# Up projection of a gated feed-forward in split float32: three matmuls per K tile, or two with the high limb of the weights over both limbs of the activations

## The chip, the cores and the metric

One NeuronCore of a Trainium2 chip runs the whole kernel in one launch. The metric is device microseconds of that core. The kernel before has a median of 1290.29 us over 3 runs (1290.16 to 1291.49).

The engines are named as in the profile: PE is TensorE (PEld its weight loads), DVE is VectorE, ACT is ScalarE, POOL is GpSimd, SP is SyncE, which here only issues DMAs.

## The reference

One layer of a hybrid attention block for 256 latent tokens and 256 context tokens of width 2048: modulation, RMSNorm, an input projection into three groups of heads, an output projection with a gated residual, then the feed-forward that matters here:

```python
h2 = rmsnorm(x, g_ffn[l]) * (1 + sc2) + sh2          # [256, 2048]
u  = h2 @ w_up[l]                                     # [256, 11264]
u  = sum(pad(u)[:, j:j + L] * conv_w[j] for j in range(3)) + conv_b   # along the tokens
gate, val = split(u, 2, axis=-1)
x  = x + gt2 * ((silu(gate) * val) @ w_down[l])       # [256, 2048]
return rmsnorm(x, g_final)
```

All inputs and the output are float32.

## The kernel before, in words

Every large matrix product is done in two limbs. `split` (L116 to L123) rounds a tile to float32r as its high limb H (ACT, L119) and takes the rest as its low limb L (DVE, L120). `mm3` (L107 to L114) then sums three products into one PSUM bank: H·H, H·L and L·H, with the first letter for the stationary side. Each of the three is a matmul of its own with a weight load of its own.

Weights arrive as raw tiles of 1 MB over SP's queue. `take` (L177 to L194) hands out a quarter of a raw tile in limbs and splits the quarters up to `look[0]` = 4 ahead of use; there are six buffers for such quarters (L161). Large tiles (raw weights, h2, gates, x2, the activations) share 16 buffers named b8 (L66). `mm3` also keeps a pace: after so many columns it calls `fill` (L272), which brings in one more 512 KB piece of the late modulation weights over POOL's queue (L217, some of them held back by a small POOL copy, L212), adds an earlier piece into a running sum on DVE (L230, L232: one pass over 128x1024), and, when a block of 16 pieces is done, sums it over the partitions on PE (L256 or L266 and L267).

Before the feed-forward, `h_cols` makes h2 from x2: transposed, scaled by gain and (1 + sc2), in limbs, but without the 1/rms of the token and without the shift. The shift stands as two more columns (L775), so that the up projection runs over 258 columns: 256 tokens and the shift's own product. `rb_make` (L782) spreads 1/rms over all partitions by two small matmuls (L787) and a copy.

The up projection has 88 column tiles of 128; a pair of them (gate and value) makes 128 columns of the activation. Per column tile there are 16 K tiles, and per K tile one `mm3` over 258 columns (L802), so 48 matmuls per column tile and 4224 in all. The first two pairs run together, K quarter by K quarter over four column tiles (`UP_FIRST`). `up_act` (L806) then takes a pair: the shift's column is copied out (DVE, L812), the product is multiplied by 1/rms (DVE, L813) and shifted (ACT, L814), convolved with three taps (L816 to L818), and silu and the product of the two halves follow (L820, L821). `store` splits the result into limbs of `act`.

The 44 pairs go in four chunks of 16, 12, 8 and 8; after each chunk the down projection takes its rows with `mm3` over 512 columns (L882). The pieces of modulation weights that are left at the feed-forward, for the second gate, are brought in during the first chunk's pairs and, at a faster pace, during its down projection; the first two column blocks of that need half of them, the last two need all (`fill_to`, L865 and L872).

The order of the instructions on each engine is fixed when the program is built, by priority and readiness, and need not be the order in which they are written.

Of the kernel before, what the change touches and what calls it, by code (L numbers as in the profile page):

```python
# [7 lines left out]
F32 = mybir.dt.float32  # L8
# [6 lines left out]
P = 128  # L15
# [13 lines left out]
UP_FIRST = 2  # L29
H_AT = 2  # L30
# [6 lines left out]
def _columns(*parts):  # L37
    """columns of the packed vectors"""
    at, o = {}, 0
    for n, w in parts:  # L40
        at[n] = (o, o + w)
        o += w
    return at, o
# [8 lines left out]
def block_kernel(ctx: ExitStack, tc: tile.TileContext, a, out):  # L52
# [54 lines left out]
    def mm3(ps, lH, lL, rH, rL, first, last, skip=False):  # L107
# [3 lines left out]
        pace[1] += pace[0] * 3 * rH.shape[-1] * 0.427e-3  # L111
# [4 lines left out]
    def split(H, L, src, scale=None):  # L116
        """H = src (* scale) rounded to float32r, L = the rest."""
# [26 lines left out]
    pace = [0.0, 0.0]  # how fast the column groups of the late mod parts follow the matrix products, and how many are due  # L144
# [10 lines left out]
    kept = [("d", (lo // 4 + q) * 4 + 3) for q in range(n // 4 - 1)]  # the last column block: rows one half after the other  # L155
# [21 lines left out]
    def take(key, i):  # L177
        """limbs of a quarter of a weight tile; later quarters are split ahead"""
# [21 lines left out]
    b2v = const.tile([P, 2, KT], F32, name="b2v")  # sh2 | sc2, per partition  # L200
# [6 lines left out]
    def m2_dma(n):  # L207
        if m2["dma"] >= len(M2):
            return
        with ExitStack() as held:  # L210
            if m2["dma"] < 4 or m2["dma"] >= 96:  # not ahead of the weights of the stage
                hold = pool.tensor_copy(tiny(1, "hold"), recent[0][:, 1, 0:1].bitcast(F32)).ins  # L212
                held.enter_context(tc.issue_after(hold))
# [7 lines left out]
    def m2_acc(flush=False):  # L221
        """what the last group brought, behind the limbs made last"""
# [14 lines left out]
    def m2_end(blk, acc):  # L237
        """limbs of a finished gate sum now, the sum over the partitions with the next group"""
# [68 lines left out]
    def mod1_mm(g):  # L307
        """sums for sh1 | sc1 of K-tile g of the stream, a quarter of the sum in every 32 rows"""
# [64 lines left out]
    # keys of the neighbourhood heads, and the first half of c_kv  # L373
# [11 lines left out]
    def proj_T(key, ps, both, part=None):  # L385
        """columns of w_in as the stationary side: [128 columns, tokens]"""
# [9 lines left out]
    def proj_N(kind, toks):  # L396
        """tokens as the stationary side: [128 tokens, 512 columns]"""
# [12 lines left out]
    # values of the neighbourhood heads  # L410
# [4 lines left out]
    # the rest of c_kv, and the rotary key  # L415
# [19 lines left out]
    # c_kv normed, in limbs  # L435
    def kv_rms():
        """1/rms of c_kv's tokens, on the diagonals of four blocks"""
# [35 lines left out]
    def softmax(S, e, scale_ap=None):  # L473
        """rows of S (PSUM or SBUF), scaled, -> their softmax"""
# [25 lines left out]
    # c_q: gain applied, in limbs; its 1/rms goes into the scale of the scores' rows  # L500
# [37 lines left out]
    # queries of the neighbourhood heads; every softmax stands between dense products  # L538
# [24 lines left out]
    # Fourier mixing  # L563
# [51 lines left out]
    # latent heads: values of four heads, queries and keys of two  # L615
# [52 lines left out]
    # the output projection's first column block starts beside the last heads  # L668
# [65 lines left out]
    def x2_cols(nb, t, gate, ss=None):  # L734
        """x2 += gate * the product, for a block of columns; sums of squares on the side"""
# [7 lines left out]
    def h_cols(nb):  # L743
        """columns of x2, transposed, gain and scale applied, in limbs; 1/rms waits until after the up projection"""
# [49 lines left out]
    def up_mm(n):  # L794
        """tiles n of the up projection, K in quarters over all of them"""
        pss = [bank() for _ in n]
        for q in range(4):
            for i, ps in zip(n, pss):
                w = take(("u", i), q)
                for k in range(4):  # L800
                    kt = 4 * q + k
                    mm3(ps[:, : SEQ + 2], w[:, 0, k * P : (k + 1) * P], w[:, 1, k * P : (k + 1) * P],  # L802
                        *hsl(h2, kt, 0, SEQ + 2), kt == 0, kt == KT - 1)
        return pss

    def up_act(j, pss):  # L806
        cv = []
        for s in range(2):
            ps = pss[s]
            c = conv[:, 2 * j + s, :]  # L810
            ub = tiny(1, "ub")
            dve.tensor_copy(ub, ps[:, SEQ : SEQ + 1])  # L812
            dve.tensor_tensor(ps[:, :SEQ], ps[:, :SEQ], rb, ALU.mult)  # L813
            act.activation(ps[:, :SEQ], ps[:, :SEQ], AF.Identity, bias=ub, scale=1.0)  # L814
# [9 lines left out]
    def finish(t):  # L824
        """1/rms, and the last columns' gain, on the rows of x2"""
# [13 lines left out]
    for ci, (lo, n) in enumerate(chunks):  # L839
        last = ci == len(chunks) - 1  # L840
        at = [b8([P, 2, 4, SEQ], F32R, s="act") for _ in range(n // 4)]
        pend = []

        def store():
            i, v = pend.pop(0)
            split(at[i // 4][:, 0, i % 4, :], at[i // 4][:, 1, i % 4, :], v)

        j = lo
        while j < lo + n:
            g = UP_FIRST if j == 0 else 1  # L850
            pss = []
            if g > 1:
                pss = up_mm(range(2 * j, 2 * j + 2 * g))
                rb_make()
            else:
                pss = up_mm([2 * j]) + up_mm([2 * j + 1])
            for i in range(g):
                v = up_act(j + i, pss[2 * i : 2 * i + 2])
# [35 lines left out]
def _layout(i):  # L894
# [5 lines left out]
    def vec(v):  # [n * 128] -> [128, n]  # L900
        return v.reshape(-1, P).T

    def tiles_k(w, k):  # [K, N] -> [K / (128 k), 128, k * N]: k K-tiles of all N columns
# [3 lines left out]
    def tiles_n(w):  # [K, N] -> [N / 128, 128, K]: all K of 128 columns  # L907
# [33 lines left out]
    # relative bias of every (head, column, row offset, key column); -1e30 outside the window  # L941
# [58 lines left out]
```

## Time and profile before

| | |
|---|---|
| median of 3 runs | 1290.29 us (1290.16 to 1291.49) |
| span of the profiled execution, first to last instruction | 1286.6 us |
| PE busy / weight loads | 1251.4 us (97%) / 1129.4 us (88%) |
| DVE busy | 982.8 us (76%) |
| ACT busy | 699.7 us (54%) |
| POOL busy | 115.0 us (9%) |
| mean granted TensorE clock | 0.994 |
| first and last matmul of the up projection | 523.1 us, 1231.4 us |

The page lists the span of the profiled execution and no device time of its own; the median stands 3.7 us above that span. Times are microseconds from the span's start. A matmul's record is longer than the distance to the next one, since matmuls are pipelined; what a matmul costs in a dense stretch is read from the distance between starts, that is from how many begin in a window. The same holds in a small way for DVE, whose records overlap by less than 0.1 us.

### The profile page before, as it was taken

The page shows a single profiled execution, that of the slowest core. Times are in us where ns is not written, and L with a number is a line of the kernel's source. Part 1 is how long each engine was busy: PE and PEld are TensorE (multiplying, and loading weights), DVE is VectorE, ACT ScalarE, POOL GpSimd, SP SyncE. Part 2 cuts the span into 40 slices and gives each one's busy share as a digit, 9 for nine tenths or more (in the row PEclk, how much of TensorE's full clock was granted, in tenths as well). Part 3 has the DMA queues.
Part 4 walks back from the last instruction along what each step waited for, and adds up shares of the span by engine and source line. Part 5 has one row for each costly group of instructions (what it writes and reads, how often), then busy time and mean ns, then how long its engine had stood idle before and what let it go on. Part 6 is the DMA issues. An engine that isn't in the chain of part 4 may idle for free.

```text
span 1286.6 us, 22194 instructions
## 1 busy us (share of the span) xinstructions
PE 1251.4 (97%) x8688; PEld 1129.4 (88%) x8688; DVE 982.8 (76%) x1805; ACT 699.7 (54%) x1327; POOL 115.0 (9%) x177
## 2 busy tenths in 40 slices
PE   5999989999999999999999999999999999999996
PEld 4888869998887888999999788999988999899985
DVE  5444588999989788798988956778766778777785
ACT  5333323765555555576666544666654566456662
POOL 0000121111111013212111100000000000000000
PEclk9999989999999999999999999999999999999998
DMA  9998688776756977766666657544455645554521
GB/s 384 419 404 317 233 291 313 239 251 240 246 196 250 363 279 293 306 255 236 227 229 230 229 196 290 184 149 164 169 192 209 243 141 193 190 207 160 189 107 66
DMA packets 53657, 304.96 MB, mean 237 GB/s; under 512 B 6064, under 2 KB 7216, under 8 KB 26800
## 3 DMA queue, kind: packets, MB, share of 16 engines
q1 hardware_dynamic: 34256, 234.37, 48.8%
q0 software_dynamic: 18432, 67.12, 15.2%
q10 hardware_dynamic: 864, 2.05, 0.4%
q8 instruction: 68, 1.11, 0.3%
q14 instruction: 37, 0.30, 0.1%
HBM read 301.42 MB, written 2.10 MB: 236 GB/s over the span
## 4 chain that ended last, share of the span: by engine, by line
PE 92%; DMA 3%; DVE 2%; ACT 1%; issue 1%; POOL 0%; DVEq 0%; POOLq 0%; ACTq 0%
PE ps L108 27%; PE ps L110 26%; PE ps L109 26%; PE g L108 2%; PE ms L314 2%; DMA wm<-in_wm_dram 2%; PE g L109 2%; PE g L110 2%; PE ps L489 1%; PE ps L360 1%; DMA sm<-in_small_dram 1%; DVE acc L232 1%; DVE hl L120 1%; PE ps L256 1%; ACT hl L119 0%
## 5 line engine op out<-in xcount | busy, mean ns | idle before, releaser
L119 ACT CAST hl<-raw 128x512 fp32r<-128x512 f32 (+2 forms) x732 | 443.6, 610 | 397.6 <-PE ps L110 315.7
L120 DVE TENSOR_TENSOR hl<-raw,hl 128x512 fp32r<-128x512 f32 (+2 forms) x732 | 486.4, 676 | 161.1 <-ACT hl L119 155.7
L108 PE MATMUL ps<-h,hl 128*128 128x258 f32 x1408 | 398.5, 283 | 0.0
L109 PE MATMUL ps<-h,hl 128*128 128x258 f32 x1408 | 396.2, 281 | 0.0
L110 PE MATMUL ps<-h,hl 128*128 128x258 f32 x1408 | 395.8, 281 | 0.0
L109 PEld LDWEIGHTS ps<-h,hl 128*128 128x128 f32 x1408 | 266.5, 189 | 0.2
L110 PEld LDWEIGHTS ps<-h,hl 128*128 128x128 f32 x1408 | 265.8, 189 | 0.0
L108 PEld LDWEIGHTS ps<-h,hl 128*128 128x128 f32 x1408 | 265.4, 189 | 0.2
L232 DVE SCALAR_TENSOR_TENSOR acc<-wm,c,acc 128x1024 f32<-128x1024 f32 x120 | 153.3, 1277 | 8.4 <-DMA wm<-in_wm_dram 8.2
L108 PE MATMUL ps<-hl,act 128*128 128x512 f32 x344 | 135.1, 393 | 0.0
L109 PE MATMUL ps<-hl,act 128*128 128x512 f32 x344 | 135.0, 393 | 0.0
L110 PE MATMUL ps<-hl,act 128*128 128x512 f32 x344 | 134.8, 392 | 0.0
L217 POOL DMA_DIRECT2D wm<-in_wm_dram x128 | 68.3, 534 | 303.1 <-DVE acc L232 225.5
L110 PEld LDWEIGHTS ps<-hl,act 128*128 128x128 f32 x344 | 64.7, 188 | 14.6
L108 PEld LDWEIGHTS ps<-hl,act 128*128 128x128 f32 x344 | 64.6, 188 | 14.3
L109 PEld LDWEIGHTS ps<-hl,act 128*128 128x128 f32 x344 | 64.7, 188 | 14.1
L212 POOL COPY hold<-hl 128x1 f32<-128x1 f32 x36 | 37.3, 1037 | 278.0 <-DVE hl L120 275.5
L817 DVE SCALAR_TENSOR_TENSOR cv<-ps,sm,cv 128x255 f32<-128x255 f32 x88 | 42.1, 481 | 24.8 <-ACT cv L816 24.4
L105 POOL TENSOR_TENSOR r<-v,mhalf 128x1 f32<-128x1 f32 (+1 forms) x3 | 4.0, 1317 | 563.1 <-DVE v L104 563.1
L816 ACT ACTIVATE cv<-ps,sm 128x256 f32<-128x256 f32 x88 | 49.5, 566 | 2.6
L108 PE MATMUL ps<-hl,mix 128*128 128x512 f32 x128 | 50.5, 394 | 0.0
L109 PE MATMUL ps<-hl,mix 128*128 128x512 f32 x128 | 50.1, 391 | 0.0
(272 smaller groups left out, 1996.1 us busy)
## 6 DMA issues: line engine op xcount, KB each, us to landing
raw<-in_wup_dram SPq DMA_DIRECT2D x88, 1024.0 KB, 4.9
wm<-in_wm_dram POOLq DMA_DIRECT2D x128, 512.0 KB, 4.8
raw<-in_wdn_dram SPq DMA_DIRECT2D x44, 1024.0 KB, 4.8
raw<-in_wm_dram SPq DMA_DIRECT2D x32, 1024.0 KB, 14.5
raw<-in_wo_dram SPq DMA_DIRECT2D x16, 1024.0 KB, 8.3
raw<-in_wB_dram SPq DMA_DIRECT2D x10, 1024.0 KB, 7.9
raw<-in_wA_dram SPq DMA_DIRECT2D x8, 896.0 KB, 14.8
x<-in_x_dram SPq DMA_DIRECT2D x4, 1024.0 KB, 8.8
```

Source lines behind the costliest of these rows:

```text
L108: pe.matmul(ps, lH, rH, start=first, stop=False, skip_group_check=skip)
L109: pe.matmul(ps, lH, rL, start=False, stop=False, skip_group_check=skip)
L110: pe.matmul(ps, lL, rH, start=False, stop=last, skip_group_check=skip)
L119: act.copy(H, src)
L120: return dve.tensor_tensor(L, src, H.bitcast(F32), ALU.subtract).ins
L212: hold = pool.tensor_copy(tiny(1, "hold"), recent[0][:, 1, 0:1].bitcast(F32)).ins
L217: pool.dma_start(w, a["wm2"][blk * 16 + kt])
L232: dve.scalar_tensor_tensor(m2["a"], w, c1[:, kt : kt + 1], m2["a"], ALU.mult, ALU.add)
L256: pe.matmul(ps[:, 2 * j : 2 * j + 2], v[:, j * P : (j + 1) * P], ones[:, 0:2], start=True, stop=True)
L314: pe.matmul(ms[r : r + 32, 0:256], cs[:, 8 * q + k, :], w[:, k, :], start=(q == 0 and k < 4), stop=(q == 1 and k >= 4), tile_position=(0, r))
L816: act.activation(t, ps[:, :SEQ], AF.Identity, bias=c[:, 3:4], scale=c[:, 1:2])
L817: dve.scalar_tensor_tensor(t[:, 1:], ps[:, : SEQ - 1], c[:, 0:1], t[:, 1:], ALU.mult, ALU.add)
```

## The change

From column pair 8 on (`UP_PLAIN = 8`), the up projection does two matmuls per K tile. The high limb of the weights meets both limbs of h in one matmul of 512 columns, so that H·H lands in the left half of a PSUM bank and H·L in the right half; the low limb of the weights meets the high limb of h in one of 256 columns. The shift's columns go: h is rebuilt with 1/rms and shift in it (`hn`), a quarter of it after every second pair of the first eight, which still run in the old way. `up_act` then adds the two halves of the bank in place of the shift and the 1/rms. `rb_make` is called after the first K quarter of the first four column tiles and not after all of them. The pace of the modulation pieces is halved during the first eight pairs. The buffers of `act` are taken one by one as they are first written.

```diff
+UP_PLAIN = 8
...
     def mm3(ps, lH, lL, rH, rL, first, last, skip=False):
...
-        pace[1] += pace[0] * 3 * rH.shape[-1] * 0.427e-3
+        paced(3 * rH.shape[-1])
+
+    def paced(n):
+        pace[1] += pace[0] * n * 0.427e-3
         if pace[1] >= 1:
             pace[1] -= 1
             fill()
...
     def up_mm(n):
...
+            if q == 0 and len(n) > 2:
+                rb_make()
         return pss
 
-    def up_act(j, pss):
+    hn = []
+
+    def hn_make(m):
+        t = sp.tile([P, 4, SEQ], F32, tag="acc", bufs=3, name=nm("hf"))
+        dve.tensor_tensor(t, h2[m][:, 0, :, :SEQ].bitcast(F32), h2[m][:, 1, :, :SEQ].bitcast(F32), ALU.add)
+        dve.tensor_tensor(t, t, rb.rearrange("p (o n) -> p o n", o=1).broadcast_to((P, 4, SEQ)), ALU.mult)
+        hn.append(b8([P, 2, 4, SEQ], F32R, s="hn"))
+        for k in range(4):
+            b = B2[:, 4 * m + k : 4 * m + k + 1]
+            H, L = hn[m][:, 0, k, :], hn[m][:, 1, k, :]
+            act.activation(H, t[:, k, :], AF.Identity, bias=b, scale=1.0)
+            dve.scalar_tensor_tensor(L, t[:, k, :], b, H.bitcast(F32), ALU.add, ALU.subtract)
+
+    def up_mm2(i):
+        ps = bank()
+        for q in range(4):
+            w = take(("u", i), q)
+            for k in range(4):
+                kt = 4 * q + k
+                h = hn[q]
+                pe.matmul(ps, w[:, 0, k * P : (k + 1) * P], h[:, :, k, :], start=kt == 0, stop=False, skip_group_check=True)
+                pe.matmul(ps[:, :SEQ], w[:, 1, k * P : (k + 1) * P], h[:, 0, k, :], start=False, stop=kt == KT - 1,
+                          skip_group_check=True)
+                paced(3 * SEQ)
+        return ps
+
+    def up_act(j, pss, plain):
...
-            ub = tiny(1, "ub")
-            dve.tensor_copy(ub, ps[:, SEQ : SEQ + 1])
-            dve.tensor_tensor(ps[:, :SEQ], ps[:, :SEQ], rb, ALU.mult)
-            act.activation(ps[:, :SEQ], ps[:, :SEQ], AF.Identity, bias=ub, scale=1.0)
+            if plain:
+                ub = tiny(1, "ub")
+                dve.tensor_copy(ub, ps[:, SEQ : SEQ + 1])
+                dve.tensor_tensor(ps[:, :SEQ], ps[:, :SEQ], rb, ALU.mult)
+                act.activation(ps[:, :SEQ], ps[:, :SEQ], AF.Identity, bias=ub, scale=1.0)
+            else:
+                lo = b1(s="lo")
+                act.copy(lo, ps[:, SEQ:])
+                dve.tensor_tensor(ps[:, :SEQ], ps[:, :SEQ], lo, ALU.add)
...
-        at = [b8([P, 2, 4, SEQ], F32R, s="act") for _ in range(n // 4)]
+        at = []
         pend = []
 
         def store():
             i, v = pend.pop(0)
+            if i % 4 == 0:
+                at.append(b8([P, 2, 4, SEQ], F32R, s="act"))
             split(at[i // 4][:, 0, i % 4, :], at[i // 4][:, 1, i % 4, :], v)
...
+            plain = j < UP_PLAIN
+            if ci == 0:
+                pace[0] = RATES["UP"] * (0.5 if plain else 1)
             if g > 1:
                 pss = up_mm(range(2 * j, 2 * j + 2 * g))
-                rb_make()
+            elif plain:
+                pss = up_mm([2 * j]) + up_mm([2 * j + 1])
             else:
-                pss = up_mm([2 * j]) + up_mm([2 * j + 1])
+                pss = [up_mm2(2 * j), up_mm2(2 * j + 1)]
             for i in range(g):
-                v = up_act(j + i, pss[2 * i : 2 * i + 2])
+                v = up_act(j + i, pss[2 * i : 2 * i + 2], plain)
+                if plain and (j + i) % 2:
+                    hn_make((j + i) // 2)
```

The rest of the diff takes out comments.

## Rows read from the trace of the kernel before

**Rows 1.** The page's head, its busy times, and the chain of work that ended last as shares of the span by engine.

```profile
span 1286.6 us, 22194 instructions
PE 1251.4 (97%) x8688; PEld 1129.4 (88%) x8688; DVE 982.8 (76%) x1805; ACT 699.7 (54%) x1327; POOL 115.0 (9%) x177
...
PE 92%; DMA 3%; DVE 2%; ACT 1%; issue 1%; POOL 0%; DVEq 0%; POOLq 0%; ACTq 0%
```

**Rows 2.** Who PE waited for, over the whole span: us in total, times, longest us.

```profile
PE ps L360 <- DVE v L104: 13.8, 1, 13.8
PE ps L266 <- ACT acl L119: 5.0, 2, 3.4
```

**Rows 3.** The page's costliest groups: the first of the three matmuls of the up projection (busy us, mean ns of a record, idle before); L109 and L110 have as many. And, from PE's order of time, the first of them.

```profile
L108 PE MATMUL ps<-h,hl 128*128 128x258 f32 x1408 | 398.5, 283 | 0.0
...
523.11 0.37 PE L108 MATMUL ps<-h,hl 128*128 128x258 f32 x1
```

**Rows 4.** PE in five dense stretches: window, its length, busy us and records that touch the window, clock, DMA share, GB/s. In order: the second chunk's up projection (1152 matmuls of 258 columns begin in it), its down projection (288 of 512), keys of a latent head (24 of 512), queries of the neighbourhood heads (96 of 256), the output projection (32 of 512). The one to three records more are those that reach over an edge.

```profile
800.20:937.70 137.50, 137.50 (x1153) 1.00 0.49 174
937.70:1003.92 66.22, 66.22 (x291) 1.00 0.59 219
397.49:403.09 5.60, 5.60 (x27) 1.00 0.87 319
246.73:257.95 11.22, 11.22 (x98) 1.00 0.81 304
515.68:522.98 7.30, 7.30 (x34) 1.00 0.97 375
```

**Rows 5.** Busy us (instructions) of PE, PEld, DVE, ACT and POOL, then clock, DMA share and GB/s. The first four rows are the time of the first eight pairs; then the start of the first down projection, a later part of it, and the second chunk's up projection.

```profile
523.00:548.00 25.00, 24.92 (x209) 24.72 (x208) 20.20 (x39) 13.44 (x28) 8.61 (x9) 1.00 0.74 285
548.00:571.00 23.00, 23.00 (x194) 23.00 (x194) 22.47 (x49) 16.98 (x35) 5.58 (x6) 1.00 0.61 227
571.00:594.00 23.00, 23.00 (x195) 23.00 (x194) 20.26 (x39) 14.59 (x29) 3.89 (x6) 1.00 0.75 256
594.00:616.00 22.00, 22.00 (x187) 22.00 (x186) 20.01 (x42) 15.44 (x31) 3.63 (x5) 1.00 0.70 260
708.00:730.00 22.00, 20.43 (x94) 16.55 (x92) 19.75 (x31) 12.02 (x23) 5.49 (x8) 1.00 0.69 238
760.00:780.00 20.00, 20.00 (x89) 16.36 (x88) 11.17 (x17) 8.97 (x15) 0.00 (x0) 1.00 0.54 188
800.00:937.00 137.00, 137.00 (x1149) 136.95 (x1148) 109.44 (x214) 88.91 (x165) 0.00 (x0) 1.00 0.49 175
```

**Rows 6.** DVE in order of time inside the first eight pairs: start us, us of the record, line.

```profile
561.43 1.27 DVE L232 SCALAR_TENSOR_TENSOR acc<-wm,c,acc 128x1024 f32<-128x1024 f32 x1
562.62 0.47 DVE L817 SCALAR_TENSOR_TENSOR cv<-ps,sm,cv 128x255 f32<-128x255 f32 x1
563.02 0.67 DVE L120 TENSOR_TENSOR hl<-raw,hl 128x512 fp32r<-128x512 f32 x1
563.62 0.47 DVE L818 SCALAR_TENSOR_TENSOR cv<-ps,sm,cv 128x255 f32<-128x255 f32 x1
```

**Rows 7.** Groups of the whole span: the instructions of `up_act` that go (L814, L812).

```profile
L814 ACT ACTIVATE ps<-ps,ub 128x256 f32<-128x256 f32 x88 | 39.2, 448 | 5.5 <-DVE ps L813 2.9
L812 DVE COPY ub<-ps 128x1 f32<-128x1 f32 x88 | 13.5, 155 | 5.2
```

**Rows 8.** Groups of DVE's instructions in two stretches: the modulation sums between 523 and 616 us, the time of the first eight pairs, and between 708.9 and 729 us, the start of the first down projection.

```profile
L232 DVE SCALAR_TENSOR_TENSOR acc<-wm,c,acc 128x1024 f32<-128x1024 f32 x12 | 15.3, 1277 | 0.0
...
L232 DVE SCALAR_TENSOR_TENSOR acc<-wm,c,acc 128x1024 f32<-128x1024 f32 x7 | 8.9, 1276 | 2.3 <-DMA wm<-in_wm_dram 2.3
```

**Rows 9.** DVE in order of time where 1/rms of x2 is made (L104) and spread on diagonals (L786).

```profile
529.75 0.16 DVE L104 TENSOR_SCALAR v<-s 128x2 f32<-128x2 f32 x1
...
532.92 0.48 DVE L786 TENSOR_SCALAR dg<-sm,r 128x128 f32<-128x128 f32 x2
```

**Rows 10.** POOL's power between the two.

```profile
530.05 2.83 POOL L105 TENSOR_TENSOR r<-v,mhalf 128x2 f32<-128x2 f32 x1 [4.82 <-DVE v L104]
```

**Rows 11.** The page's GB/s in 40 slices of 32.2 us each.

```profile
GB/s 384 419 404 317 233 291 313 239 251 240 246 196 250 363 279 293 306 255 236 227 229 230 229 196 290 184 149 164 169 192 209 243 141 193 190 207 160 189 107 66
```

**Rows 12.** The chain that ended last, in order of time, where the last modulation piece arrives.

```profile
719.50 8.46 DMA wm<-in_wm_dram
...
728.05 1.30 DVE acc L232
```

**Rows 13.** PE where the sum of the last block of pieces stands.

```profile
728.03 0.40 PE L110 MATMUL ps<-hl,act 128*128 128x512 f32 x1
730.05 0.51 PE L266 MATMUL ps<-acl,ones_r 128*128 128x512 f32 x1 [1.62 <-ACT acl L119]
```

**Rows 14.** PE in order of time around its longest wait after the start (in brackets: idle before, and for whom).

```profile
179.67 0.40 PE L110 MATMUL ps<-hl,hx 128*128 128x512 f32 x1
183.46 0.80 PE L266 MATMUL ps<-acl,ones_r 128*128 128x512 f32 x1 [3.39 <-ACT acl L119]
```

**Rows 15.** PE in the stretch behind that wait, and in one behind the shorter wait at 730 us: length, busy (records), granted clock.

```profile
183.50:189.40 5.90, 5.90 (x13) 0.50 0.73 244
732.00:740.00 8.00, 8.00 (x36) 1.00 0.63 242
```

**Rows 16.** From the view of the running sum's tile: 16 matmuls of two columns in a row, each with a load of 128 columns (min, median, max ns; first and last start).

```profile
L256 PE MATMUL ps<-ones_r,acc x16: 165/251/251, 513.7 to 515.2; 128*128 128x2 f32 x16
```

## The prediction, made before the changed kernel ran

> **What bounds it now.** I read the page's busy times and the chain first, then who PE waited for, then the distance between matmuls stage by stage. PE is busy for 97% of the span and makes up 92% of the chain [rows 1]; it waited 13.8 us once, at the start, and 5.0 us in two places for a modulation sum [rows 2]. So PE's own stream is the time, and the up projection is its largest piece: 1408 matmuls on each of three lines [rows 3]. Records overlap, so prices come from starts: 1152 matmuls of 258 columns in 137.50 us are 119.4 ns each, 288 of 512 columns in the down projection 229.9 ns, 24 of 512 with weights stationary and activations moving 233.3 ns, 96 of 256 columns 116.9 ns, 32 of 512 in the output projection 228.1 ns [rows 4]. A K tile of the up projection is 3 x 119.4 = 358.2 ns. Second in line is DVE: in the first eight pairs it is busy 20.20, 22.47, 20.26 and 20.01 us of 25, 23, 23 and 22, which leaves 10.1 us of 93 idle; in the second chunk it is idle for 20% [rows 5].
>
> **The pair of matmuls.** 36 column pairs of 44 change: 72 column tiles x 16 = 1152 K tiles. The new pair moves 768 columns where the old three moved 774. No row shows a 512-column matmul between 256-column ones, nor a moving operand in two runs of 256, so I bound it. The 512 columns: 228.1 at best, 233.3 at worst by the rows; I take 231.6, midway between the nearest by form (233.3, weights stationary) and the nearest by place (229.9, between the same up projections). The 256 columns: 116.9 at best, 119.4 at worst; I take 118.5, which is 119.4 less two columns at 0.45 ns (229.9 / 512). Sum 350.1, saving 8.1 ns per K tile, 9.3 us in all. The ends are 345.0 (13.2 ns, 15.2 us) and 352.7 (5.5 ns, 6.3 us). The saving may also vanish, if the two runs cost (a rival).
>
> The Trainium skill, in "TensorE: Matmul & The Clock Gate", section Back-to-back issue gap, has another price: it gives columns / 2.4 GHz plus 2.5 ns for a warm matmul. By it the old three would be 330 ns and the new two 325, an estimate of 5.0 ns per K tile and 5.8 us in all. The trace disagrees on its own shapes: 119.4 and 229.9 ns stand where the rule has 110.0 and 215.8, and what is over the columns grows with them.
>
> **Rebuilding h.** Four `hn_make`, one after every second pair of the first eight. On DVE each has two passes over 128x1024 and four over 128x256. By starts a pass over 1024 takes 1.19 us (561.43 to 562.62) and one over 256 0.39 to 0.40 [rows 6]: 2 x 1.19 + 4 x 0.39 = 3.9 us, 15.8 us for four. ACT's four passes each (0.45 us in L814's size [rows 7], 7 us in all) fit: ACT is busy for about two thirds of that time [rows 5]. Against it the halved pace takes out about 6 of the 12 modulation sums in this stretch [rows 8], 6 x 1.19 = 7.1 us. Room is 10.1 + 7.1 = 17.2 us for 15.8: it fits, with 1.4 us to spare in 93, so DVE would be full. What hides it is the split-ahead: four quarters of weights, 4 x 4 x 0.358 = 5.7 us of matmuls, more than one `hn_make`. That DVE's order is not the written one but packed by readiness is seen where a weight split stands between two passes of one activation [rows 6]. The last quarter is the tight one: it is written behind pair 7's activation, and PE wants it 12 K tiles into pair 8, 4.2 us later. I take 1.5 us of PE wait for the stage; the ends are 0 and, with no idle time usable, 15.8 - 7.1 = 8.7.
>
> **1/rms earlier.** PE would reach its two small matmuls after 48 matmuls of the first quarter, 5.7 us after 523.1 [rows 3] and some transposes, about 529.4 us. The diagonals they need are done at 532.92 + 0.48 = 533.4 [rows 9], behind a POOL power of 2.83 us [rows 10]. Placed literally it costs 4.0 us and holds up the whole PE queue; placed by readiness nothing. I take 0.5 us; ends 0 and 4.0.
>
> **The modulation pieces.** The code calls for 0.132 x 774 x 0.427e-3 = 0.0436 of a piece per K tile; 256 K tiles at half of that are 5.6 pieces fewer before the down projection. There 7 are left now [rows 8] and 12 to 13 after, each with a place every 2.46 us (the pace's 3.56 products of 0.69 us), so the last moves from 20 us into it to 32. DVE: the down projection alone has it at 56% [rows 5], 32 x 0.56 + 13 x 1.19 = 33.4 us for 32, full again. DMA: 1 MB per 5.5 us plus half a MB per 2.46 us is 404 GB/s, and no slice of the run has over 419 [rows 11]. Today the last piece takes 8.46 us to land [rows 12] and PE sits from 728.03 to 730.05 for its sum [rows 13]. The second gate's last columns are wanted 43 us in, so nothing else queues for it, but the sum stands in PE's own order. I take 0.5 us more than today's wait of about 1.8 us; ends -2 (the wait goes) and +6.
>
> **The rest.** Per pair of tiles, a 0.155 us DVE copy goes, and an ACT pass of 0.448 becomes a copy of as many columns [rows 7]: off the path, nothing. Both h2 and hn hold b8 buffers until pair 8, leaving three or four for raw weights, each used for 5.7 us: nothing, since two in flight give 11 us against landings of 8.46 us at the slowest shown [rows 12].
>
> **Sum.** 9.3 - 1.5 - 0.5 - 0.5 = 6.8 us. The profiled span is 1286.6 us [rows 1], its forecast 1279.8; the median of the runs stands 3.7 us above that span, and I carry this over: 1283.5. One thing is not linear: behind a wait of 3.8 us [rows 14] PE ran at half its clock, 1.2 GHz, for 5.9 us [rows 15], which costs up to 3.0 us; behind the 2.0 us wait at 730 it did not.
>
> **Rivals.** (a) *Only columns count.* If weight loads bind the old stream, the third load goes as well. For it: in the up projection PEld is busy 136.95 of 137.00 us, in the down projection 16.36 of 20 [rows 5], and 16 tiny matmuls with loads start over 1.5 us, so a load alone holds a place for about 0.10 us [rows 16]. Against: 119.4 is still above that. The best rows give 345.0, 15.2 us: 1290.3 - 15.2 + 2.5 = 1277.6. The Trainium skill, in "Perfetto Trace Analysis", section Identifying the Most-Contended Engine, judges TensorE's headroom by the load row and not by matmul busy time; by that rule this rival would hold.
>
> (b) *A small fixed price per matmul is all that goes.* With the worst rows, 233.3 + 119.4: 6.3 us saved, 1290.3 - 6.3 + 2.5 = 1286.5. The Trainium skill's gap rule above would come out here.
>
> (c) *The change does not pay on PE.* If the moving operand's two runs are taken like two matmuls, 2 x 119.4 + 118.5 = 357.3: 1.0 us saved, against 2.5 lost, 1291.8. For it: no row has two runs. Against: each run is 256 long.
>
> (d) *Slower: DVE falls behind in the first eight pairs.* Its room is 1.4 us. If its idle time, which stands in pieces behind ACT, cannot be used, PE waits 8.7 us, and with one fall of the clock 3.0 more: 1290.3 - 9.3 + 8.7 + 3.0 + 1.0 = 1293.7. It decides from about 12 us of waits on; for it DVE's 22.47 of 23 [rows 5], against it that PE did not wait there.
>
> **How the numbers follow.** About 0.2% (2.6 us) is what a measurement here can tell from no change. Forecast 1283.5: 0.48, own range 1280 to 1288 (nearly all faster); (a) 0.15, faster; (b) 0.14, faster in two thirds; (c) 0.11, same but for 0.02 slower; (d) 0.12, slower but for 0.02 same. Faster 0.47 + 0.15 + 0.09 = 0.71, same 0.01 + 0.05 + 0.09 + 0.02 = 0.17, slower 0.12. The range goes from (a) less the wait that may vanish, 1276, to 1291, which leaves out most of (d) and half of (c).
>
> **What would show it.** Right: 2304 matmuls on the two new lines, about 350 ns per K tile in a dense chunk, so the second chunk's up projection 134.4 us instead of 137.5; PE waits under 3 us between 523 and 620 us; DVE nearly full there. Wrong: a K tile at 357 or at 345; a PE wait before the 512-column matmul for hn of the last quarter; a stretch at half clock after 523 us; a wait over 4 us for the last modulation sum.

## The result, and the profile after

The changed kernel takes 1279.27 us (median of 4 runs, 1278.86 to 1282.86) against 1290.22 (4 runs, 1284.76 to 1291.49): ratio 0.9932, 95% interval [0.9911, 0.9953]. That is faster, by 10.95 us. It lies inside the outer range of 1276 to 1291 and 0.7 us below the range of 1280 to 1288 that went with the main account; the forecast of 1283.5 was 4.2 us too high. Run again beside other kernels it took 1279.72 us, ratio 0.9921 [0.9893, 0.9950]. The profiled run took 1279.01 us, 1.8 us more than its span, and all other profiled runs with a time of their own stand 1.7 to 1.8 us over their spans. So before's profiled run, with 1286.6 us of span, took about 1288.4 (an estimate from these differences), not the 1290.3 of its median.

The page after: the head, the busy times and the chain's shares by engine, which answer to [rows 1].

```profile
span 1277.2 us, 19956 instructions
PE 1243.7 (97%) x7536; PEld 1069.2 (84%) x7536; DVE 978.6 (77%) x1757; ACT 699.0 (55%) x1343; POOL 111.5 (9%) x177
...
PE 90%; DMA 3%; DVE 3%; issue 1%; ACT 1%; POOL 0%; DVEq 0%; ACTq 0%; POOLq 0%
```

PE is still the bound; DVE's share of the chain rose from 2% to 3%. The new pair in the list of costly groups, 1152 times each, as announced (busy, mean ns of a record, idle before):

```profile
L834 PE MATMUL ps<-hn,hl 128*128 128x512 f32 x1152 | 404.3, 395 | 0.0
L835 PE MATMUL ps<-hn,hl 128*128 128x256 f32 x1152 | 323.4, 281 | 0.0
```

The second chunk's up projection, which answers to the first line of [rows 4] and the last of [rows 5]: first the kernel before, then after, each cut at the first and last start of the stage. Columns: window, length, busy us (records) of PE, PEld, DVE, ACT, POOL, clock, DMA share, GB/s.

```profile
800.19:937.59 137.40, 137.40 (x1153) 137.40 (x1152) 109.71 (x215) 89.00 (x165) 0.00 (x0) 1.00 0.49 174
...
797.73:932.32 134.59, 134.59 (x768) 117.52 (x767) 102.80 (x192) 86.48 (x165) 0.00 (x0) 1.00 0.51 177
```

That is 134.59 / 384 = 350.5 ns per K tile instead of 137.40 / 384 = 357.8. Note PEld: it was solid before and now has 17 us free. By distances between starts the 512-column matmul takes 233.1 ns on average and the 256-column one 117.7. Their sum is 350.8 and not 350.5, because a stage measured from its first to its last start lacks one matmul; with it the two prices are 350.8 and 358.1, and the difference is the same 7.3.

The stages, from the first to the last start of their matmuls, us:

```
                 up 1   down 1  up 2   down 2  up 3   down 3  up 4   down 4
before          185.70  91.02  137.40  65.98   91.58  44.00   91.58  44.17
after           183.86  91.58  134.59  66.90   89.68  44.11   89.70  43.65
difference       -1.84  +0.56   -2.81  +0.92   -1.90  +0.11   -1.88  -0.52
```

The four up projections give 8.43 us, which is 1152 K tiles at 7.3 ns: nothing of it was lost to waits. The down projections take back 1.07. The first matmul starts 1.17 us earlier (521.94 instead of 523.11), and what follows the last is 0.84 shorter. In sum 9.4 us, the difference of the spans.

Not all of this comes back in other runs. The changed kernel run again and its two shifted copies (experiments 8 to 11) start the up projection between 521.3 and 523.2 us and spend 89.9 to 90.6 us in the first down projection; the shifted copy of before starts at 525.3 and spends 90.4 there. So the start and the first down projection are scatter. What recurs in all of them is 8.4 us from the up projections, 0.5 us lost in the three later down projections, and the 0.8 us at the end: 8.8 us.

The first eight pairs and the stretch behind them (columns as above), against the first four lines of [rows 5]:

```profile
522.00:547.00 25.00, 24.92 (x209) 24.72 (x208) 24.90 (x46) 14.51 (x30) 6.08 (x7) 1.00 0.64 232
547.00:570.00 23.00, 23.00 (x195) 23.00 (x195) 22.48 (x51) 19.66 (x42) 0.83 (x3) 1.00 0.52 186
570.00:593.00 23.00, 23.00 (x195) 23.00 (x194) 22.94 (x49) 16.47 (x33) 2.36 (x3) 1.00 0.37 128
593.00:616.00 23.00, 23.00 (x193) 22.91 (x192) 20.81 (x42) 16.48 (x34) 2.23 (x3) 1.00 0.62 214
616.00:640.00 24.00, 24.00 (x139) 20.94 (x138) 21.53 (x40) 16.25 (x32) 3.25 (x6) 1.00 0.89 345
```

DVE is busy for 91.1 us of the first 94, and PE pauses once, for 0.08 us, as it did before. Who PE waited for, over the span (us in total, times, longest), against [rows 2], the first two lines:

```profile
PE ps L364 <- DVE v L105: 13.6, 1, 13.6
PE ps L270 <- ACT acl L123: 3.8, 2, 2.9
```

### The profile page after: what moved, and what is told of

Its sections match the earlier page's. It is cut to its first block, busy times and chain, and to the rows that moved or that the text cites. A ratio compares the mean times of both kernels' runs of the same rounds, so it can differ in the third digit from the quotient of the medians.

```text
span 1277.2 us, 19956 instructions
## 1 busy us (share of the span) xinstructions
PE 1243.7 (97%) x7536; PEld 1069.2 (84%) x7536; DVE 978.6 (77%) x1757; ACT 699.0 (55%) x1343; POOL 111.5 (9%) x177
## 4 chain that ended last, share of the span: by engine, by line
PE 90%; DMA 3%; DVE 3%; issue 1%; ACT 1%; POOL 0%; DVEq 0%; ACTq 0%; POOLq 0%
PE ps L834 21%; PE ps L109 16%; PE ps L110 15%; PE ps L111 15%; PE ps L835 11%; DMA wm<-in_wm_dram 3%; PE g L109 2%; PE ms L318 2%; PE g L110 2%; PE g L111 2%; DVE acc L236 1%; DVE hl L124 1%; PE ps L493 1%; PE ps L364 1%; DMA sm<-in_small_dram 1%
## 5 line engine op out<-in xcount | busy, mean ns | idle before, releaser
L834 PE MATMUL ps<-hn,hl 128*128 128x512 f32 x1152 | 404.3, 395 | 0.0
L835 PE MATMUL ps<-hn,hl 128*128 128x256 f32 x1152 | 323.4, 281 | 0.0
L834 PEld LDWEIGHTS ps<-hn,hl 128*128 128x128 f32 x1152 | 216.4, 188 | 51.2
L835 PEld LDWEIGHTS ps<-hn,hl 128*128 128x128 f32 x1152 | 217.1, 188 | 0.2
L236 DVE SCALAR_TENSOR_TENSOR acc<-wm,c,acc 128x1024 f32<-128x1024 f32 x120 | 153.6, 1280 | 8.7 <-DMA wm<-in_wm_dram 8.4
L110 PE MATMUL ps<-hl,act 128*128 128x512 f32 x344 | 135.7, 394 | 0.5 <-DVE hl L124 0.5
L109 PE MATMUL ps<-hl,act 128*128 128x512 f32 x344 | 135.2, 393 | 0.0
L110 PEld LDWEIGHTS ps<-hl,act 128*128 128x128 f32 x344 | 64.7, 188 | 15.9 <-DVE hl L124 1.5
L109 PEld LDWEIGHTS ps<-hl,act 128*128 128x128 f32 x344 | 64.6, 188 | 14.9
L109 PE MATMUL ps<-h,hl 128*128 128x258 f32 x256 | 72.5, 283 | 0.0
L111 PE MATMUL ps<-h,hl 128*128 128x258 f32 x256 | 72.1, 282 | 0.0
L110 PE MATMUL ps<-h,hl 128*128 128x258 f32 x256 | 72.1, 282 | 0.0
L109 PE MATMUL ps<-hl,mix 128*128 128x512 f32 x128 | 50.5, 394 | 0.0
L110 PE MATMUL ps<-hl,mix 128*128 128x512 f32 x128 | 50.1, 391 | 0.0
L111 PE MATMUL ps<-hl,mix 128*128 128x512 f32 x128 | 49.9, 390 | 0.0
```

Of the source, the lines that this page charges most:

```text
L109: pe.matmul(ps, lH, rH, start=first, stop=False, skip_group_check=skip)
L110: pe.matmul(ps, lH, rL, start=False, stop=False, skip_group_check=skip)
L111: pe.matmul(ps, lL, rH, start=False, stop=last, skip_group_check=skip)
L236: dve.scalar_tensor_tensor(m2["a"], w, c1[:, kt : kt + 1], m2["a"], ALU.mult, ALU.add)
L834: pe.matmul(ps, w[:, 0, k * P : (k + 1) * P], h[:, :, k, :], start=kt == 0, stop=False, skip_group_check=True)
L835: pe.matmul(ps[:, :SEQ], w[:, 1, k * P : (k + 1) * P], h[:, 0, k, :], start=False, stop=kt == KT - 1, skip_group_check=True)
```

## Experiments

"Pair" is the two matmuls of a K tile, and a K tile's price is the second chunk's up projection over 384. The first matmul of the up projection starts anywhere between 521.1 and 528.0 us in the profiled runs, so prices are compared stage by stage.

**1. Three matmuls over the rebuilt h.** The halves of the bank stay; only the merging is undone.

```diff
-                pe.matmul(ps, wH, h[:, :, k, :], ...)                # 512 columns
-                pe.matmul(ps[:, :SEQ], wL, h[:, 0, k, :], ...)
+                pe.matmul(ps[:, :SEQ], wH, h[:, 0, k, :], ...)       # 256 columns each
+                pe.matmul(ps[:, SEQ:], wH, h[:, 1, k, :], ...)
+                pe.matmul(ps[:, :SEQ], wL, h[:, 0, k, :], ...)
```

> The changed kernel with three matmuls of 256 columns per K tile from pair 8 on, where it has one of 512 and one of 256; the rebuilt h, the two halves of the bank and what adds them stay as they are. It splits the gain (358.2 to about 350.8 ns per K tile) into its two parts: two columns fewer per matmul, and one matmul fewer. Theory of the prediction (what goes is mostly a matmul's own price; 256 columns cost 118.5 ns): 3 x 118.5 = 355.5 ns per K tile, 4.7 ns x 1152 = 5.4 us slower than the changed kernel. Rival 1 (the two extra columns were all of it; 256 columns cost 117 ns, as in the neighbourhood heads' queries): 351 ns, the same time as the changed kernel within 0.5 us. Rival 2 (a weight load binds, whatever the columns): 3 x 119.4 = 358 ns, 8.5 us slower.

Measured: 1280.72 us, ratio 0.9936 [0.9910, 0.9962].

```profile
797.05:932.62 135.57, 135.57 (x1153) 135.57 (x1151) 102.77 (x192) 86.61 (x165) 0.00 (x0) 1.00 0.50 177
```

353.0 ns per K tile. With three matmuls as before, 4.8 of the 7.3 ns are already there; merging two of them adds 2.5. So at these places most of the gain is not in the merge.

**2. The same with one half and no addition in the epilogue.**

```diff
-                pe.matmul(ps[:, SEQ:], wH, h[:, 1, k, :], ...)
+                pe.matmul(ps[:, :SEQ], wH, h[:, 1, k, :], ...)
...
-                lo = b1(s="lo")
-                act.copy(lo, ps[:, SEQ:])
-                dve.tensor_tensor(ps[:, :SEQ], ps[:, :SEQ], lo, ALU.add)
```

> As the one with three matmuls of 256 columns, but all three sum into one half of the bank, so that nothing has to be added after (an ACT copy and a DVE pass of 256 columns fewer per column tile). Theory of the prediction: PE's price is that of the other kernel with three matmuls, 355.5 ns, and the lighter DVE and ACT give nothing back, as PE did not wait for them: 5.4 us slower than the changed kernel. Rival 1 (only the two columns counted): 351 ns and the time of the changed kernel within 0.5 us; if DVE or ACT cost anything there, faster by up to 1 us.

Measured: 1282.08 us, 0.9944 [0.9924, 0.9965]; the second chunk's up projection again 135.57 us. The epilogue on ACT and DVE costs PE nothing, as the prediction had it.

**3. The 512 moving columns in one run.**

```diff
-        hn.append(b8([P, 2, 4, SEQ], F32R, s="hn"))
+        hn.append(b8([P, 4, 2, SEQ], F32R, s="hn"))
```

> The changed kernel with the two limbs of the rebuilt h next to each other for each K tile, so that the 512 moving columns are one run and not two of 256. Theory of the prediction: the two runs cost nothing; 512 columns stay at 233 ns, the pair at 350 to 351 ns, the same time within 0.5 us. Rival (two runs cost something at the seam): 512 columns fall to the down projection's 229.9 ns, 3.2 ns x 1152 = 3.7 us faster.

Measured: 1280.14 us, 0.9940 [0.9918, 0.9962]; stage 134.59 us, matmuls 233.1 and 117.7 ns, all as after. Two runs of 256 cost nothing: rival (c) falls.

**4. 256 columns of the 258.** The kernel before, its h untouched, with rows 258 apart. It leaves out the shift's product.

```diff
-                    mm3(ps[:, : SEQ + 2], ..., *hsl(h2, kt, 0, SEQ + 2), kt == 0, kt == KT - 1)
+                    mm3(ps[:, :SEQ], ..., *hsl(h2, kt, 0, SEQ), kt == 0, kt == KT - 1)
```

> The kernel before with the two columns of the shift left out of the up projection's matmuls (256 columns out of rows of 258, all three matmuls in one half; the shift's own product is not computed and a stand-in is added in its place). It tells whether two columns or the place of the rows in memory make up the 119.4 ns of 258 columns. Theory of the prediction: 118.5 ns per matmul, 3.8 us less over 4224 matmuls. Rival 1 (the columns themselves, beyond their 0.45 ns): 117 ns, 10 us less. Rival 2 (it is the rows, which start at odd places): 119 ns, the same time.

Measured: one run, 1287.49 us, span 1285.7.

```profile
800.06:937.06 137.00, 137.00 (x1152) 137.00 (x1151) 106.11 (x192) 86.30 (x165) 0.00 (x0) 1.00 0.49 175
```

356.8 ns per K tile: six columns less are worth 1.0 ns, not the 2.7 that 0.45 ns a column would give.

**5. Rows 260 apart.** The kernel before, so that each row of h starts at a multiple of 16 bytes. The shared buffers grow by 64 bytes with it.

```diff
-    h2 = [b8([P, 2, 4, SEQ + 2], F32R, s="h2") for _ in range(4)]
+    h2 = [b8([P, 2, 4, SEQ + 4], F32R, s="h2") for _ in range(4)]
```

> The kernel before with the rows of h2 260 elements apart and not 258, so that each row starts at a multiple of 16 bytes; still three matmuls of 258 columns. In the kernel before, K tiles with odd row number (their rows start at 8 bytes past a multiple of 16) take 360.0 ns and those with even number 356.3 ns. Theory (the place of the rows is a good part of what h rebuilt gains): all K tiles fall to 356 ns, 1.9 to 2.2 ns x 1408, 2.6 to 3.1 us less over the up projection. Rival (the rows don't matter; odd and even differ by chance of the order): 358.2 ns as before, no change over 0.5 us.

Measured: one run, 1294.57 us; its up projection starts 4.9 us later than before's (527.98).

```profile
805.98:944.11 138.13, 138.13 (x1152) 138.12 (x1151) 109.70 (x215) 88.94 (x165) 0.00 (x0) 1.00 0.48 171
```

359.7 ns per K tile, slower than before, so rows that start at multiples of 16 bytes do not by themselves bring the lower price. (The other large tiles moved with the larger buffers, and what that does was not separated.) The Trainium skill, "SBUF — State Buffer", section Door 1: The DMA port swizzle, says that SBUF is read in lines of 16 bytes and that each crossing to a new one has a price. This run shows no such price for where a matmul's rows start.

**6. The full pace of the modulation pieces.**

```diff
-                pace[0] = RATES["UP"] * (0.5 if plain else 1)
+                pace[0] = RATES["UP"]
```

> The changed kernel without the halved pace of the modulation pieces in the first eight pairs: about 5.6 pieces more there, 6.7 us of DVE, where DVE has 2.9 us of 94 idle. Theory (DVE is full there and the halved pace is what makes room for the rebuilt h): PE waits 2 to 5 us between 522 and 620 us; the 1.9 us of waits in the first down projection go, as 7 and not 13 pieces are left for it; 0 to 3 us slower in sum. Rival (the weights split ahead and the order by readiness take it up): no wait of PE before 620 us, and 1 to 2 us faster in sum.

Measured: one run, 1285.56 us; its up projection starts 3.8 us later than after's. The first up projection takes 184.45 us, 0.6 more than after: the waits of several us did not come. The only wait of PE there is at the early `rb_make`, and the one for the last modulation sum grew (PE in order of time; in brackets idle before and for whom; the lines between left out):

```profile
534.65 0.71 PE L791 MATMUL ps<-dg,ones_r 128*128 128x128 f32 x4 [0.34 <-DVE dg L790]
...
731.98 0.50 PE L270 MATMUL ps<-acl,ones_r 128*128 128x512 f32 x1 [2.92 <-ACT acl L123]
```

With 8 pieces left and not 13, the last sum came 21.7 us into the down projection and not 36, but PE waited longer for it, and that stage took 93.91 us. So halving the pace, which the prediction needed to make room on DVE, bought only 0.6 us there, and in this one run 2.3 to 3.5 us in the down projection, against after's 91.58 and its repeat's 90.37.

**7. The rebuild in four pairs instead of eight.**

```diff
-UP_PLAIN = 8
+UP_PLAIN = 4
...
-                    hn_make((j + i) // 2)
+                    hn_make(j + i - 1)
+                    hn_make(j + i)
```

> The changed kernel with four and not eight column pairs in the old way: two quarters of h rebuilt after pair 1 and two after pair 3. 128 more K tiles in the new way, 128 x 7.4 ns = 0.9 us gained on PE. Theory (DVE is the limit of how early h can be rebuilt): in the first 48 us DVE is busy for 47.4 with two quarters, the other two are 7.8 us more, so PE waits 3 to 7 us before pair 5 and the kernel is 2 to 6 us slower; one wait over 3.5 us would bring a stretch at half clock, 2 to 3 us more. Rival (the split-ahead covers it): no wait, 0.9 us faster.

Measured: one run, 1288.99 us. The first up projection takes 187.17 us, 3.3 more than after, though four more pairs run as matmul pairs, and the first down projection 97.75 instead of 91.58. PE in order of time:

```profile
554.40 0.39 PE L109 MATMUL ps<-h,hl 128*128 128x258 f32 x1 [1.94 <-ACT hl L123]
555.16 0.39 PE L111 MATMUL ps<-h,hl 128*128 128x258 f32 x1 [0.25 <-DVE hl L124]
...
736.88 1.32 PE L270 MATMUL ps<-acl,ones_r 128*128 128x512 f32 x2 [5.46 <-ACT acl L123]
```

This is rival (d) seen alive: with the rebuild packed twice as close the weight limbs come late. Eight pairs are enough, four are not.

**8 to 11. All tiles 32 or 64 bytes further on.** Experiments 1 to 5 left the suspicion that a matmul's price hangs on where its tiles lie.

```diff
+    const.tile([P, 8], F32, name="gap")        # 16 for 64 bytes
     sm = const.tile([P, SM_W], F32, name="sm")
```

> The kernel after with every SBUF tile 32 bytes further on (a tile of 8 unused numbers ahead of the others). Theory (4.9 of the 7.4 ns that a K tile gained belong to the places of the new tiles, not to the merge): the pair moves away from 350.8 ns by 1 to 6 ns either way, which is 0.3 to 1.7 us in a stage of 288 pairs (second chunk's up projection 134.59 us), and the 256-column matmul leaves 117.7 ns by up to 3. Rival (the price belongs to the number of columns alone): 233.1 and 117.7 ns again, up projection 134.6 us within 0.1.

> The kernel before with every SBUF tile 32 bytes further on. Theory (place): the 258-column matmul leaves 119.4 ns by 0.5 to 3 ns either way, the second chunk's up projection 137.40 us by 0.6 to 3.5 us. Rival (columns alone): 119.4 ns and 137.4 us within 0.1.

> The kernel after with every SBUF tile 64 bytes further on. Theory (place, by the address within 64 bytes): the prices of the kernel after return, 350.8 ns a pair within 0.3, if what counts repeats every 64 bytes; if it repeats over a longer stretch, the pair lies elsewhere than both 350.8 and the pair 32 bytes on. Rival (columns alone): 350.8 ns in all three.

> The kernel after once more, beside the three shifted ones: 350.8 ns a pair and 134.6 us for the second chunk's up projection by every theory; the time 1279.3 us within 3 us, as far as the stretch before the up projection differs from run to run.

Measured: after + 32 bytes 1278.60 us (0.9916 [0.9885, 0.9947]), after + 64 bytes 1277.78 (0.9916 [0.9883, 0.9948]), after again 1279.72; before + 32 bytes 1289.25, ratio to before 1.0003 [0.9981, 1.0024]. The same stage, one line from each of the three shifted kernels:

```profile
798.02:932.62 134.60, 134.60 (x769) 117.52 (x768) 102.80 (x192) 86.48 (x165) 0.00 (x0) 1.00 0.51 177
```

```profile
796.22:930.81 134.59, 134.59 (x768) 117.52 (x767) 102.77 (x192) 86.44 (x165) 0.00 (x0) 1.00 0.50 175
```

```profile
801.71:939.10 137.39, 137.39 (x1152) 137.39 (x1151) 109.74 (x215) 89.01 (x165) 0.00 (x0) 1.00 0.49 174
```

Not 0.1 us moves. My theory fell in this form: moving everything together by 32 or 64 bytes changes nothing. What these runs leave open is how the tiles lie inside and to each other.

**12. Rows of 256, end to end.** The kernel before with three matmuls, no rebuild, h at the places of before, but without the gap of two columns between its rows. Like experiment 4 it leaves out the shift's product.

```diff
-    h2 = [b8([P, 2, 4, SEQ + 2], F32R, s="h2") for _ in range(4)]
+    h2t = [b8([P, 2064], F32R, s="h2") for _ in range(4)]
+    h2 = [h[:, :2048].rearrange("p (l k n) -> p l k n", l=2, k=4) for h in h2t]
```

> The kernel before with three 256-column matmuls per K tile, h in rows of 256 one against the other at the places of the four h tiles, the two columns of the shift behind the rows (the shift's product with the weights is left out of the sum). Theory (rows of 256 one against the other, as hn has them, are worth the 3.75 ns that lie between 119.03 ns, rows 258 apart, and 117.78 ns, hn): 117.8 ns a matmul, 353.4 a K tile, second chunk's up projection 135.6 us. Rival (it is hn's four places against the other operands): 119.0 ns, 357.1 a K tile, 137.0 us. Between them, each has a share.

Measured: 1283.14 us, ratio 0.9940 [0.9922, 0.9959]; its first matmul of the up projection starts 3.2 us later than after's.

```profile
801.58:936.04 134.46, 134.46 (x1153) 134.46 (x1152) 106.00 (x192) 86.33 (x165) 0.00 (x0) 1.00 0.50 178
```

350.2 ns per K tile, with three matmuls and three loads: as good as the pair's 350.5. Against experiment 4, where the same matmuls over as many columns took 356.8, the one edit is the distance between the rows. It is worth 6.6 ns, more than the 3.75 that I had left for it. Over the four up projections the kernel takes 496.98 us, the changed one 497.83, the one before 506.26.

The mean price of a matmul by the quarter of h that it reads, ns between starts, from 745 us on (the last column: K tile in the second chunk):

```
                                        q0      q1      q2      q3     K tile
before, 258 columns, rows 258 apart   118.65  121.19  118.28  119.42   357.8
exp. 4, 256 columns, rows 258 apart   118.77  120.00  118.89  118.47   356.8
exp. 12, 256, rows 256 apart          117.77  117.84  117.77  113.90   350.2
exp. 1, 256, rows 256 apart, hn       118.85  114.94  118.40  118.94   353.0
after, the 256 of the pair, hn        117.10  117.11  117.08  119.33   350.5
after, the 512 of the pair, hn        236.13  231.92  233.96  230.62
```

The table also sets limits to that reading. Half of the 6.6 ns, 3.4, falls on the last quarter alone (118.47 to 113.90). Experiment 1 has rows end to end as well, and in three of its four quarters a matmul costs 118.4 to 118.9 ns, about as much as in experiment 4. And the first row of each quarter's high limb lies at the same place with the same numbers in experiments 4 and 12, yet the matmuls over it took 119.7 and 117.4 ns. So the distance between the rows moves the price at these places, but a row's own place does not tell its price, and rows end to end do not always have the lower one.

## Why the prediction was right, and where not

**The price of the K tile was right, by luck in part: more than half of the reason was wrong.** The text forecast 350.1 ns, and 350.5 came; the 8.1 ns saved were 7.3, 8.4 us in all instead of 9.3. The two terms: 233.1 ns where I took 231.6, close to the worst row of 233.3 [rows 4], and 117.7 where I took 118.5, so their errors partly cancelled. And I drew the gain from merging (238.8 to 231.6) and from two columns at 0.45 ns. The runs say otherwise:
- The six columns themselves give 1.0 ns (experiment 4).
- Laying the rows of h end to end gives 6.6 ns (12 against 4), at the old places and without a merge. I had put this term at nothing, without a reason.
- The move from h to the rebuilt `hn`, at other places and with other numbers in it, costs 2.9 ns with three matmuls (353.0 against 350.2). Experiment 7's `hn` holds the same numbers, written earlier; its K tile took 351.3 ns, and its 512-column matmuls 234.9, 230.6, 236.2 and 232.1 ns by quarter, other prices than after's. So the numbers alone do not set the price; whether they have a share was not separated.
- Merging gives 2.5 ns there (353.0 to 350.5).

1.0 + 6.6 - 2.9 + 2.5 = 7.2, the 7.3 but for rounding. These are steps along one path through the experiments, so their sum is no check, and another path would divide the 4.8 ns of the first three differently. What stands is that the merge is worth 2.5 ns, 2.9 us in all, and that measured only at hn's places, while the other 4.8 come from replacing h by `hn`. That this is because the shift's two columns no longer stand between the rows is likely from experiment 12 and not shown for hn's places. I found the 256-column row of the neighbourhood heads at 116.9 ns [rows 4] before predicting, used it as a bound, and did not ask why it lay 2.5 ns under 119.4.

**Rebuilding h: mechanism right, cost 0 instead of 1.5 us.** The forecast was that DVE would be full with 1.4 us to spare; 2.9 of 94 us were idle. DVE's groups between 522 and 616 us (records, busy us, mean ns) show the parts, against [rows 8]:

```profile
L236 DVE SCALAR_TENSOR_TENSOR acc<-wm,c,acc 128x1024 f32<-128x1024 f32 x7 | 9.0, 1280 | 0.0
L824 DVE SCALAR_TENSOR_TENSOR hn<-hf,B,hn 128x256 fp32r<-128x256 f32 x16 | 7.2, 480 | 0.0
...
L817 DVE TENSOR_TENSOR hf<-h 128x1024 f32<-128x1024 f32 x4 | 4.9, 1219 | 0.0
L818 DVE TENSOR_TENSOR hf<-hf,rb 128x1024 f32<-128x1024 f32 x4 | 4.9, 1218 | 0.0
```

Four rebuilds are 17.0 us by records, where I had 15.8 by starts; seven sums stayed, against my six. The split-ahead that I named as cover held: PE did not wait, and experiments 6 and 7 show where its edge is.

**1/rms earlier: 0 instead of 0.5 us.** The first of its small matmuls ran at 530.38 us without a wait. At full pace it cost 0.3 us.

**The modulation pieces: the count as forecast, the wait not.** 13 pieces stand in the down projection (12 to 13 forecast). The chain in order of time, and PE where it waits, answer to [rows 12, 13]:

```profile
719.97 9.90 DMA wm<-in_wm_dram
...
731.54 6.60 DMA wm<-in_wm_dram
...
741.47 0.63 ACT acl L123
...
742.14 0.50 PE ps L270
```

```profile
734.30 0.50 PE L110 MATMUL ps<-hl,act 128*128 128x512 f32 x1 [0.31 <-DVE hl L124]
...
742.14 0.50 PE L270 MATMUL ps<-acl,ones_r 128*128 128x512 f32 x1 [0.88 <-ACT acl L123]
```

The sum came 36 us into the down projection (32 forecast) and the wait for it shrank to 0.88 us, but DVE, full again, made PE wait for weight limbs too, 0.31 us here. I had forecast the wait for the sum to grow by 0.5 us. The stage is 0.56 us longer, but that this meets the 0.5 is luck: run again, the same kernel took 90.37 us there, less than before's 91.02.

**What the sum lacked.** The second down projection, untouched, grew by 0.92 us. Its matmuls cost what their act tile makes them cost: 227.66, 229.17 and 232.88 ns for the three tiles before, 232.81, 233.21 and 233.24 after, 96 of each: 9.55 x 96 = 0.92 us. Taking the buffers of act later probably puts them in other slots; no run separates this. The start and the end gave 2.0 us that no step foresaw; 1.2 of it, at the start, is scatter, and why the end is shorter stays open. And I carried 3.7 us over the span to a run that stood 1.8 over its own; that is 1.9 of the 4.2 us. By spans, 9.4 against 6.8: pair -0.9, rebuild +1.5, 1/rms +0.5, down projections -0.6, start and end +2.0, which is 2.5 of 2.6. The profiled run itself was 0.3 us under its median, which makes 4.2.

**The rivals.** (a) failed: a K tile took 350.5, not 345. That the loads bind falls twice: with one load gone PEld has 13% free and the price falls by only 2.5 ns, and in experiment 12 three loads fill the row at 350.2 ns as they did at 357.8. A record of a load is 188 to 189 ns long in all three kernels, longer than the 117 to 119 ns from one start to the next, so three loads per K tile make the row solid at any of these prices; within the 233.1 ns of a 512-column matmul such a record leaves 45 ns, and 384 x 45 ns is about the 17 us of free time. The Trainium skill ("Perfetto Trace Analysis", Identifying the Most-Contended Engine) judges TensorE's headroom by its share of peak FLOPs and by the busy share of weight loads; the second of these, read alone as in the prediction, misleads here, since a solid load row still let 7.6 ns go (busy us, mean ns, idle before; before, experiment 12, after).

```profile
L109 PEld LDWEIGHTS ps<-h,hl 128*128 128x128 f32 x1408 | 266.5, 189 | 0.2
...
L110 PEld LDWEIGHTS ps<-h,hl 128*128 128x128 f32 x1408 | 264.8, 188 | 0.0
...
L834 PEld LDWEIGHTS ps<-hn,hl 128*128 128x128 f32 x1152 | 216.4, 188 | 51.2
```

(b) is closest for the merge by itself: 2.5 ns. The Trainium skill's gap of 2.5 ns a matmul ("TensorE: Matmul & The Clock Gate", Back-to-back issue gap), which that section gives for an isolated matmul, agrees with that one difference, and not with the absolute prices, nor with experiment 12. (c) fell with experiment 3. (d) did not come with eight pairs and did with four.

**Open.** Why rows 1032 bytes apart cost more than rows 1024 apart, and rows 1040 apart no less, and why the gain is so uneven over the quarters; whether a merge at the old places of h would go below 350.2; what in the relation of two tiles moves a 512-column matmul between 227 and 233 ns. None of the runs beat the changed kernel by more than the interval.

## What to carry to other kernels

Before a gain is credited to fewer instructions, run the many with the new layout: here three matmuls, on rows laid end to end, were at one place as fast as the two, and at another 2.5 ns slower. Columns appended to each row of a moving operand may cost more than their own width, so try them in a tile of their own. And when a full engine gets new work, ask what runs ahead of the bound engine: here weights split four quarters ahead let 17 us of rebuilding pass on a DVE with 3 us of 94 left, and PE did not wait.

## What the runs showed of the hardware

- A matmul's price is exact to 0.1 us per stage from run to run in the second to fourth chunks, and the same with a lighter epilogue on DVE and ACT (135.57 us in both experiments 1 and 2). Yet it differs by tile: 113.9 to 120.0 ns for 256 columns, 227.7 to 233.2 for 512 by the stationary act tile, 230.6 to 236.1 by the moving quarter of hn. Moving everything together by 32 or 64 bytes leaves it as it is.
- Waits of 2.13 us and more were followed by half the clock. In experiment 12 PE waited 2.14 us before 729.22 us, and the stretch behind ran at 1.2 GHz (length, busy and records per engine, granted clock):

```profile
730.20:733.40 3.20, 3.20 (x9) 2.42 (x9) 2.68 (x6) 0.63 (x2) 0.00 (x0) 0.50 0.83 317
```

  So it was in experiment 3 behind 2.13 us at 184 us and in experiments 4, 6 and 7 behind 2.84, 2.92 and 5.46 us in the first down projection. Behind the kernel before's wait of 1.62 us [rows 13, 15], after's of 0.88 us and experiment 7's of 1.94 us at 554 us it stayed at 2.4 GHz. The length of the wait does not decide alone: in experiment 5 the clock was at half at 32 us, behind a wait of 1.70 us in a stretch with other pauses, and in experiment 7 a wait of 1.70 us at 184 us cost nothing of it:

```profile
32.10:35.20 3.10, 3.10 (x16) 3.10 (x16) 0.00 (x0) 0.00 (x0) 0.00 (x0) 0.50 1.01 418
...
184.50:190.00 5.50, 5.27 (x21) 3.94 (x22) 5.50 (x9) 1.60 (x3) 0.94 (x3) 1.00 0.78 276
```
